# Issuing four of seven input loads late, from between GpSimd's row sums, in a sparse 3x3 convolution

## Chip, cores, metric

The kernel runs on one core of one Trainium2 chip. The metric is the device time of one execution in microseconds (us), as the median of several runs. A run is called fast or slow by its state: a slow run is over 1.5% above the fastest of the same kernel. Only fast runs enter a ratio; a median and its range are over all runs of a kernel, and where a slow one is among them the text says so.

## The reference

The convolution takes 16 images of 64 channels and 64x64 pixels, and 128 filters of 3x3 with one weight in ten kept. Everything is float32.

```
x_pad = np.pad(x, ((0, 0), (0, 0), (1, 1), (1, 1)))
for b, co, ci, kh, kw:
    if weight[co, ci, kh, kw] != 0:
        output[b, co] += weight[co, ci, kh, kw] * x_pad[b, ci, kh:kh+64, kw:kw+64]
```

The input is 16.8 MB, the weights 0.3 MB, and the output 33.6 MB. The kernel does not use the zeros; it computes a dense product in bf16.

## The kernel before

Two images form a pair, which fills 128 partitions (2 x 64 channels). There are 8 pairs, each in its own tile `xs[p]`, so a load never waits for a buffer to come free. GpSimd issues the loads because they cast float32 to bf16 on the way. Here all of them are issued at the start:

```python
    xs = [x_pool.tile([128, H, W], BF16, name=f"x{p}") for p in range(NP)]
    ...
    nc.sync.dma_start(out=x_head[:, 0:HEAD, :], in_=pair(0)[:, 0:HEAD, :])
    nc.gpsimd.dma_start(out=xs[0][:, HEAD:H, :], in_=pair(0)[:, HEAD:H, :])
    ...
    for p in range(1, NP):
        nc.gpsimd.dma_start(out=xs[p], in_=pair(p))

    ...                                   # idle matmuls, ahead of the first real ones
    for _ in range(27):
        nc.tensor.matmul(idle_ps, idle_rhs, idle_rhs, start=True, stop=True)
```

The first half of pair 0, the "head", comes as float32 through SyncE's queue and is cast by VectorE and ScalarE. A pair has 4 blocks of 16 rows. In 31 of the 32 blocks GpSimd first adds neighbouring rows (a "row sum"), TensorE multiplies, ScalarE and VectorE put the parts together in an output tile `o`; only pair 0's first block goes without a row sum. SyncE then stores the pair:

```python
    def twos(p, o, r0):
        s = s_pool.tile([128, 8, W], BF16, name="s")          # 3 buffers
        nc.gpsimd.tensor_tensor(out=s, in0=xs[p][:, r0 : r0 + 16 : 2, :],
                                in1=xs[p][:, r0 + 1 : r0 + 16 : 2, :], op=ADD)
        shared = product([(s, G1, 0, 1)], 8)
        ...
    for p in range(NP):
        o = [o_pool.tile([C_OUT, H, W], FP32, name="o") for _ in range(2)]   # 7 buffers
        last = p == NP - 1
        for blk in range(4):
            ...
                twos(p, o, r0)
            ...                    # of the last pair, each half is stored by itself
        if not last:
            for n in range(2):
                nc.sync.dma_start(out=out[2 * p + n], in_=o[n])
```

## Time and profile before

| what | value | where from |
|---|---|---|
| time | 127.82 us (127.75 to 128.02, 4 runs) | runs |
| span of the profiled run | 125.4 us (this run took 127.12 us) | page |
| TensorE, VectorE, GpSimd busy | 86%, 66%, 32% | page |
| the 16 DMA engines busy with q1 and q0 | 96.9% | page |
| last addition of VectorE ends | 111.8 us | chain of waits |
| last store has landed | 124.2 us | landing records |

The page is the summary of one profiled execution. In its lines PE is TensorE, PEld TensorE's loading of weights, DVE VectorE, ACT ScalarE, POOL GpSimd and SP SyncE; a q behind the name means the engine's instruction queue. L135 is line 135 of the kernel, `s<-x` writes tile `s` and reads tile `x`, and x36 counts instructions. PEclk, or the granted clock, is the share of TensorE's full clock that it was given.

The two queues are q1, which SyncE feeds (stores, weights, head), and q0, which GpSimd feeds (casting loads). One more view is needed: the page's list of transfers, with the size of each (an output store counted in float32, a load on its bf16 side) and the median time in us from issue to landing.

```profile
out_dram<-o SPq DMA_DIRECT2D x14, 2048.0 KB, 19.8
x<-in_x_dram POOLq DMA_DIRECT2D x7, 1024.0 KB, 29.3
out_dram<-o SPq DMA_DIRECT2D x4, 1024.0 KB, 12.3
```

A store of 2 MB takes some 5 us alone (an estimate: 2.1 MB at 421 GB/s, the rate over this whole kernel), yet 19.8 us pass from its issue: transfers stand in a queue.

### The profile page before, as it was taken

How to read it: one execution, taken by the hardware profiler on the slowest of the kernel's cores; microseconds unless marked ns; L12 is line 12 of the kernel's file. 1: busy time of each engine (PE TensorE's matmuls, PEld its weight loads, DVE VectorE, ACT ScalarE, POOL GpSimd, SP SyncE). 2: the span in 40 equal slices, each digit the busy share in tenths (PEclk: the TensorE clock that was granted, in tenths of full speed). 3: DMA queues.
4: the chain of work that ended last, by engine and by line, in shares of the span. 5: the costliest groups of instructions: out<-in, count | busy, mean ns of one | idle time of the engine just before them, and what ended most of it. 6: DMA issues, size and time to landing. Idle time of an engine off the chain costs nothing.

```text
span 125.4 us, 2486 instructions
## 1 busy us (share of the span) xinstructions
PE 107.5 (86%) x1002; PEld 58.8 (47%) x1002; DVE 82.4 (66%) x135; ACT 39.0 (31%) x71; POOL 40.7 (32%) x45
## 2 busy tenths in 40 slices
PE   6679999999999999999999999999999999920000
PEld 6435555555555555555555555555555555500000
DVE  0463877877787778777877787778777877760000
ACT  4555323333333333333333333333333333300000
POOL 6936533333333333333333333333333300000000
PEclk9999999999999999999999999999999999997555
DMA  5999999989999999999999999999999999999980
GB/s 146 338 222 220 212 214 220 191 259 350 324 311 337 308 293 319 342 316 308 426 429 423 408 429 434 450 416 434 418 418 429 429 444 423 434 397 423 423 369 10
DMA packets 4044, 42.93 MB, mean 342 GB/s; under 512 B 448, under 2 KB 448, under 8 KB 704
## 3 DMA queue, kind: packets, MB, share of 16 engines
q1 hardware_dynamic: 2880, 34.90, 66.2%
q0 software_dynamic: 1152, 7.86, 30.7%
q8 instruction: 8, 0.13, 0.4%
q14 instruction: 4, 0.03, 0.1%
HBM read 17.07 MB, written 33.55 MB: 404 GB/s over the span
## 4 chain that ended last, share of the span: by engine, by line
PE 81%; DMA 4%; DVE 1%; issue 1%; DVEq 0%; SPq 0%
PE ps L135 81%; DMA o<-in_x_dram 4%; DVE o L168 1%; DVEq L214 0%; DVE x L87 0%; SPq L60 0%; DVEq L168 0%
## 5 line engine op out<-in xcount | busy, mean ns | idle before, releaser
L168 DVE TENSOR_TENSOR o<-ps,pc 128x512 f32<-128x512 f32 x124 | 77.8, 686 | 22.1 <-PE ps L135 19.8
L135 PE MATMUL ps<-x,wT 64*128 64x504 bf16 (+3 forms) x780 | 88.8, 373 | 1.5 <-DVE x L87 1.5
L135 PEld LDWEIGHTS <-wT 64*128 64x128 bf16 x966 | 55.2, 94 | 49.4 <-issue 1.5
L154 POOL TENSOR_TENSOR s<-x 128x512 bf16<-128x512 bf16 x31 | 35.6, 1152 | 57.7 <-PE ps L135 41.5
L161 ACT COPY pc<-ps 128x512 f32<-128x512 f32 x62 | 33.3, 589 | 64.0 <-issue 61.8
L135 PE MATMUL ps<-s,wT 64*128 64x512 bf16 (+1 forms) x186 | 25.7, 377 | 0.0
L74 PE MATMUL ps<-idle_rhs 128*128 128x128 bf16 x27 | 3.1, 310 | 1.0 <-DVE idle_rhs L71 1.0
L67 POOL DMA_DIRECT2D x<-in_x_dram x7 | 3.7, 561 | 0.0
L74 PEld LDWEIGHTS <-idle_rhs 128*128 128x128 bf16 x27 | 2.8, 144 | 1.0 <-DVE idle_rhs L71 1.0
L91 DVE CAST w_bf<-w_sb 128x192 bf16<-128x192 f32 (+1 forms) x4 | 1.3, 382 | 3.0 <-DMA w_sb<-in_weight_dram 3.0
L149 DVE COPY o<-ps 128x512 f32<-128x512 f32 x2 | 1.4, 692 | 2.0 <-PE ps L135 2.0
L148 ACT COPY o<-ps 128x512 f32<-128x512 f32 x2 | 1.2, 586 | 2.4 <-PE ps L135 2.4
L87 ACT CAST x<-o 128x576 bf16<-128x576 f32 (+1 forms) x2 | 1.5, 802 | 0.5 <-DMA o<-in_x_dram 0.5
L91 ACT ACT_TABLE_LOAD x1 | 1.3, 1283 | 0.7 <-PEq L203 0.7
L97 PE MATMUL ps<-ident,w_bf 128*128 128x128 bf16 x9 | 1.1, 292 | 0.4 <-DVE w_bf L91 0.4
L87 DVE CAST x<-o 128x576 bf16<-128x576 f32 x1 | 0.5, 460 | 1.4 <-DMA o<-in_x_dram 1.4
L91 ACT CAST w_bf<-w_sb 128x64 bf16<-128x64 f32 (+1 forms) x2 | 0.7, 418 | 1.9 <-DMA w_sb<-in_weight_dram 1.9
L97 PEld LDWEIGHTS <-w_bf 128*128 128x128 bf16 x9 | 0.8, 128 | 0.8 <-DVE w_bf L91 0.8
L101 DVE TENSOR_TENSOR wT<-ps,wT 128x384 bf16<-128x384 f32 x2 | 1.0, 550 | 0.0
L63 POOL DMA_DIRECT2D x<-in_x_dram x1 | 0.7, 696 | 0.8 <-POOLq L203 0.8
L71 DVE MEMSET idle_rhs<- 128x64 uint32 x1 | 0.1, 112 | 0.8 <-PEq L203 0.8
L110 ACT CAST wT<-ps 128x384 bf16<-128x384 f32 x1 | 0.5, 481 | 0.4 <-PE ps L97 0.4
(8 smaller groups left out, 1.9 us busy)
## 6 DMA issues: line engine op xcount, KB each, us to landing
out_dram<-o SPq DMA_DIRECT2D x14, 2048.0 KB, 19.8
x<-in_x_dram POOLq DMA_DIRECT2D x7, 1024.0 KB, 29.3
out_dram<-o SPq DMA_DIRECT2D x4, 1024.0 KB, 12.3
o<-in_x_dram SPq DMA_DIRECT2D x1, 1024.0 KB, 5.4
x<-in_x_dram POOLq DMA_DIRECT2D x1, 512.0 KB, 7.5
w_sb<-in_weight_dram SPq DMA_DIRECT2D x1, 288.0 KB, 3.1
```

Of the source, the lines that this page charges most:

```text
L67: nc.gpsimd.dma_start(out=xs[p], in_=pair(p))
L74: nc.tensor.matmul(idle_ps, idle_rhs, idle_rhs, start=True, stop=True)
L87: copy(out=xs[0][:, a:b, :], in_=x_head[:, a:b, :])
L91: copy(out=w_bf4[:, g, a:b, :], in_=w_v[:, k : k + b - a, :])
L97: nc.tensor.matmul(wps[:, j, :], src, ident, start=True, stop=True)
L101: nc.vector.tensor_tensor(out=wT[:, g], in0=wps, in1=wT[:, G1], op=SUB)
L135: nc.tensor.matmul(ps[n][:, lo:hi, c_lo:c_hi], tap(g, kw, n), src[q, a:b:step, c_lo + kw - 1 : c_hi + kw - 1], start=(i == 0), stop=(i == ...
L148: nc.scalar.copy(out=o[0][:, r0 : r0 + rows, :], in_=ps[0])
L149: nc.vector.tensor_copy(out=o[1][:, r0 : r0 + rows, :], in_=ps[1])
L154: nc.gpsimd.tensor_tensor(out=s, in0=xs[p][:, r0 : r0 + 16 : 2, :], in1=xs[p][:, r0 + 1 : r0 + 16 : 2, :], op=ADD)
L161: nc.scalar.copy(out=c, in_=shared[n])
L168: nc.vector.tensor_tensor(out=o[n][:, first : r0 + 16 : 2, :], in0=ps[n], in1=pc[n], op=ADD)
```

## The change

The intent is to let the first stores have the DMA engines to themselves: pairs 4 to 7, which nobody needs before about 50 us, are no longer loaded at the start. Each is loaded while the pair three places ahead of it is computed.

```diff
-    for p in range(1, NP):
+
+    def load(p):
         nc.gpsimd.dma_start(out=xs[p], in_=pair(p))
+
+    EARLY = 4
+    for p in range(1, EARLY):
+        load(p)
@@ in the loop over pairs and blocks
                 twos(p, o, r0)
+                if p > 0 and blk == 1 and p + EARLY - 1 < NP:
+                    load(p + EARLY - 1)
```

## The prediction

> **What bounds the kernel now.** I read the page first: the span, the busy rows, the DMA queues.
>
> ```profile
> span 125.4 us, 2486 instructions
> ...
> PE   6679999999999999999999999999999999920000
> ...
> DMA  5999999989999999999999999999999999999980
> ...
> q1 hardware_dynamic: 2880, 34.90, 66.2%
> q0 software_dynamic: 1152, 7.86, 30.7%
> ...
> HBM read 17.07 MB, written 33.55 MB: 404 GB/s over the span
> ```
>
> TensorE looks like the bound, full from slice 4 to slice 36. But its row ends at about 112 us, and the DMA row is full from slice 2 to slice 39. The queue shares say it in one number: q1 (SyncE's transfers) and q0 (GpSimd's) together keep the 16 DMA engines busy for 96.9% of the span, 121.5 of 125.4 us. The chain of waits, in order of time, ends like this (start, length, what):
>
> ```profile
> 7.12 102.09 PE ps L135 x954
> ...
> 111.16 0.60 DVE o L168
> ```
>
> The chain stops at 111.76 us and the span at 125.4: in the last 13.6 us no engine computes, and only stores drain. The page's "PE 81%" follows the computation to the last issue of a store; it doesn't say what delayed that store's landing. Next I cut the span into stretches of 3 us. Columns: stretch, length, busy time (count) of PE, its weight loads, DVE, ACT, POOL; then granted clock, DMA share, GB/s.
>
> ```profile
> 15.00:18.00 3.00, 3.00 (x30) 1.60 (x28) 2.27 (x5) 1.07 (x2) 1.15 (x1) 1.00 1.04 216
> ...
> 36.00:39.00 3.00, 3.00 (x32) 1.57 (x29) 2.27 (x5) 1.07 (x2) 1.16 (x1) 1.00 1.04 333
> ...
> 66.00:69.00 3.00, 3.00 (x31) 1.60 (x28) 2.27 (x5) 1.07 (x2) 1.15 (x1) 1.00 1.03 437
> ...
> 114.00:117.00 3.00, 0.00 (x0) 0.00 (x0) 0.00 (x0) 0.00 (x0) 0.00 (x0) 0.59 1.01 426
> ```
>
> The DMA share is 1.0 in every stage: loads alone (15 us), loads beside stores (36), stores alone with TensorE running (66), stores alone after it (114). The rates look different only because q0 casts float32 to bf16 and its bytes are counted on the bf16 side: 7.86 MB in q0 stand for 15.7 MB read. Counted on the float32 side, 216 is 432 GB/s, like the 426 to 437 of the stores. So one resource is full at one rate from start to end, and **the time is set by the DMA engines' total work**. TensorE would matter only if it left them without work.
>
> The work: 50.63 MB in HBM bytes. The share of 0.43 in the first stretch (0 to 3 us) puts its start at about 1.7 us, that of 0.62 in 120 to 123 its end at about 121.9. That is 120.2 us, 421 GB/s, or 2.374 us for each MB. The last landing record, at 124.2 us, comes 2.3 us later, then the program's end.
>
> **What the Trainium skill says.**
> - "DMA: Bandwidth & Descriptors", section "Issuing engines are not separate DMA queues": transfers started by different engines run on the same 16 DMA engines and interleave. The trace agrees: in the packet records of 36 to 60 us a 16 KB packet takes 624 ns on either queue, and the two together move about 422 GB/s, what one moves alone. Moving a load from early to late gives stores bandwidth earlier and takes as much away later.
> - The same page, section "Measured": a 16 MB load reaches 425 GB/s. Here 421 over the whole kernel: no rate is left to gain by a better order.
> - "Perfetto Trace Analysis", section "Per-instruction lifecycle: what the profiler-reported window actually captures": for a GpSimd transfer the profiled interval ends with the descriptors, not with the data. The trace agrees: 561 ns for each issue, 29.3 us median to landing.
> - "SBUF — State Buffer", section "SBUF: two separate sides", the box on VectorE and GpSimd's descriptors: a two-port VectorE instruction keeps GpSimd from writing them. The four moved issues will stand beside L168, a two-input addition from PSUM, not one of the copies that the box warns of. No issue of the kernel before stands beside L168, so its trace is silent here.
>
> **The change part by part.** GpSimd's instruction order in the built kernel confirms the diff: after three row sums of pair 0 and two of pair 1 comes the load of pair 4, then the loads of 5, 6, 7, each after the second row sum of pairs 2, 3, 4. Nothing is removed or added: 8 issues and 31 row sums remain, and TensorE's, VectorE's and ScalarE's work is the same. When would the loads be issued? GpSimd's timeline in the kernel before (start, length, what, idle before):
>
> ```profile
> 13.77 1.15 POOL L154 TENSOR_TENSOR s<-x 128x512 bf16<-128x512 bf16 x1 [2.21 <-DMA x<-in_x_dram]
> 15.16 1.15 POOL L154 TENSOR_TENSOR s<-x 128x512 bf16<-128x512 bf16 x1 [0.23 <-PE ps L135]
> 18.40 1.15 POOL L154 TENSOR_TENSOR s<-x 128x512 bf16<-128x512 bf16 x1 [2.09 <-PE ps L135]
> ...
> 27.97 1.15 POOL L154 TENSOR_TENSOR s<-x 128x512 bf16<-128x512 bf16 x1 [2.10 <-PE ps L135]
> ```
>
> The row at 13.77 is pair 1's first block, that at 15.16 its second, so load 4 goes out at 15.16 + 1.15 = 16.3 us. Pair 2's second is at 27.97 (load 5 at 29.1), pairs 3 and 4 follow 12.8 us apart (41.9 and 54.7).
> - GpSimd: 4 x 0.56 us leave the start, where it then idles 2.0 us anyway waiting for ScalarE's cast, and come back one at a time in front of row sums with 2 us of idle time before them. Worth 0.
> - Deadlines: the row sums that first read pairs 4 to 7 start at 50.3, 63.1, 75.9 and 88.8. A load is 2.10 MB, 5 us alone, 10 us at half share. Load 4 should land near 30, the others near 41, 54, 67. At least 20 us to spare: TensorE won't wait.
> - DMA: does it ever run dry? I add up issued work. A pair's load is 4.98 us, a pair's stores (4.19 MB) 9.96. Up front: weights and pairs 0 to 3, 8.68 MB, 20.6 us, from 1.7 to 22.3. Stores of a pair are issued at 21.6 and then every 12.8 us, as now; the last pair's two halves at 104.7 and 111.2.
>
> ```
> issued at    what        work is queued until   left just before
>  16.3        load 4       27.3                   6.0
>  21.6        stores 0     37.2                   5.7
>  29.1        load 5       42.2                   8.1
>  34.4        stores 1     52.2                   7.8
>  41.9        load 6       57.1                  10.3
>  47.2        stores 2     67.1                   9.9
>  54.7        load 7       72.1                  12.4
>  60.0        stores 3     82.0                  12.1
>  72.8        stores 4     92.0                   9.2
>  85.6        stores 5    101.9                   6.4
>  98.4        stores 6    111.9                   3.5
> 104.7        last, half  116.9                   7.2
> 111.2        last, half  121.9                   5.7
> ```
>
> The queue is never empty, and the smallest margin (3.5 us at 98.4) is there before the change too, since all loads have landed by then in both. The end is 121.9, as now. **Sum: 0 us.** What changes is only who lands first: the stores of pairs 0 to 2 some microseconds earlier, loads 4 to 7 later.
>
> **The rivals.**
> 1. *TensorE sets the end, and earlier stores shorten the tail.* For it: the 81%, and loads that no one needs for 30 us compete with the first stores. Were it true, the last stores (2.1 MB, 5 us) would start when issued, at 111.2, and land near 118.5: 5.7 us gained, 122.1 us. Against it: the 5.7 us of older stores queued at 111.2, which no order of loads removes.
> 2. *A DMA hole opens.* The first stores, issued at 21.6, move their first packet only at 25.8 by the packet records. If load 4 came late, the engines would stand from 22.3 to 25.8: up to 3.5 us lost, 131.3 us, slower by 2.7%. Against it: load 4 is issued 6 us before its turn and carries the engines to 27.3. A smaller hole, in single engines, I allow 0.5 us.
> 3. *Switching costs or gains.* From 23.5 to 26 us the packet records sum to 330 KB less than at 430 GB/s, 0.8 us. If several separate loads each bring such a dip, up to +2 us; if none does, -0.8.
> 4. *GpSimd's issue is slowed beside VectorE.* Even 5 us for an issue would only use the margin before row sums that lie 2 blocks ahead; nothing or almost nothing.
>
> **Range and chances.** My best guess is the time before, 127.82 us, plus 0.1 for rivals 2 and 3 taken together: 127.9. Runs of before spread over 0.2 us; with -0.8 and some +1 for the dips the range is 127.1 to 128.9. Over 2% faster needs below 125.3, which rival 1 alone could give: 0.03. Over 2% slower needs above 130.4, a full hole of rival 2 or many dips: 0.04. Within 2%: 0.93.
>
> **What would show it.** Right: DMA share 1.0 in every stretch from 3 to 120 us; the two queues' shares again sum to about 97%; TensorE's chain piece of about 102 us unchanged, with no wait on a load of x; GpSimd's issues in pairs 1 to 4 near 0.56 us each; loads land in a median of about 11 us instead of 29.3, whole-image stores in about 18 instead of 19.8; the last landing still 12 to 13 us after the last store is issued. Wrong: a stretch of DMA share well below 1 near 22 to 30 us (rival 2), a DMA total in us that grew (rival 3), or a span that ends nearer to TensorE's end (rival 1).

## The result

The changed kernel took 127.31 us (127.09 to 127.56, 4 runs), the kernel before 127.82 us. The ratio is 0.9958, with a 95% interval of 0.9937 to 0.998. Ratios here are the mean time of one kernel's fast runs over that of the other's in the same rounds, so they are not quite the ratio of the medians quoted. By the 2% rule the time is the same.

The page of the changed kernel, in the rows shown of before:

```profile
span 125.5 us, 2486 instructions
...
PE   6669999999999999999999999999999999990000
...
DMA  4999999999999999999999999999999999999980
...
q1 hardware_dynamic: 2880, 34.90, 66.3%
q0 software_dynamic: 1152, 7.86, 30.6%
...
HBM read 17.07 MB, written 33.55 MB: 403 GB/s over the span
```

The DMA row is as full as it was, and the queues' shares sum to 96.9% again. But the PE row reaches one slice further. The chain of waits of the changed kernel (start, length, what) tells by how much:

```profile
7.50 104.60 PE ps L141 x954
...
114.04 0.60 DVE o L174
```

TensorE's piece of the chain ended at 109.2 us before and ends at 112.1 now, and VectorE's last addition ends at 114.6 instead of 111.8. **Computation ended 2.9 us later, and the span is the same within 0.2 us.** The last landing is at 124.4 us (124.2 before). That alone says what kind of kernel this is: the tail of stores after the computation has shrunk by what the computation lost.

The delay is not spread out. GpSimd's timeline (start, length, what, idle before) shows the first late load and its neighbours:

```profile
18.05 1.15 POOL L160 TENSOR_TENSOR s<-x 128x512 bf16<-128x512 bf16 x1 [2.09 <-PE ps L141]
19.14 0.57 POOL L68 DMA_DIRECT2D x<-in_x_dram  x1
21.30 1.14 POOL L160 TENSOR_TENSOR s<-x 128x512 bf16<-128x512 bf16 x1 [1.59 <-PE ps L141]
```

The issue takes 0.57 us out of idle time: the next row sum had 1.59 us of idle time left before it, where others have 2.0 to 2.1. So GpSimd is not what came late. TensorE's timeline from its start shows it, first of the kernel before, then of the changed kernel:

```profile
4.46 1.12 PE L97 MATMUL ps<-ident,w_bf 128*128 128x128 bf16 x9 [0.41 <-DVE w_bf L91]
7.12 3.99 PE L135 MATMUL ps<-x,wT 64*128 64x512 bf16 x36 [1.54 <-DVE x L87]
```

```profile
4.21 1.22 PE L103 MATMUL ps<-ident,w_bf 128*128 128x128 bf16 x9 [0.16 <-DVE w_bf L97]
7.50 6.49 PE L141 MATMUL ps<-x,wT 64*128 64x512 bf16 x36 [2.07 <-DVE x L93]
```

The same first 36 products took 3.99 us before and 6.49 us now: TensorE started slowly, after standing idle for 2.07 instead of 1.54 us, and computed 2.5 us late from there on. (The other 0.4 us of the 2.9 are its later start, 7.50 instead of 7.12 us.) The list of waits has no load of x in it, for TensorE or for GpSimd.

Finally the list of transfers, and one stretch of 3 us (columns as in the prediction; the last two are DMA share and GB/s), both of the changed kernel:

```profile
out_dram<-o SPq DMA_DIRECT2D x14, 2048.0 KB, 15.9
x<-in_x_dram POOLq DMA_DIRECT2D x7, 1024.0 KB, 16.1
out_dram<-o SPq DMA_DIRECT2D x4, 1024.0 KB, 9.6
```

```profile
99.00:102.00 3.00, 3.00 (x34) 1.55 (x30) 2.48 (x4) 0.91 (x3) 0.99 (x2) 1.00 0.90 377
```

Stores land earlier after their issue and loads sooner after theirs, as they must if each waits behind less. In this stretch the DMA share is 0.90, against 1.01 in the kernel before: the queue of stores ran nearly dry, because pair 6's stores came 3 us late. (With the same order of loads and these stores on time, `after_warm` below loses nothing there.)

### The profile page after: what moved, and what is told of

It reads as the page before. It is cut to its first block, busy times and chain, and to the rows that moved or that the text cites. A ratio compares the mean times of both kernels' runs of the same rounds, so it can differ in the third digit from the quotient of the medians.

```text
span 125.5 us, 2486 instructions
## 1 busy us (share of the span) xinstructions
PE 110.1 (88%) x1002; PEld 57.2 (46%) x1002; DVE 82.3 (66%) x135; ACT 38.9 (31%) x71; POOL 40.6 (32%) x45
## 4 chain that ended last, share of the span: by engine, by line
PE 83%; DMA 5%; DVE 1%; issue 1%; DVEq 0%; SPq 0%
PE ps L141 83%; DMA o<-in_x_dram 5%; DVE o L174 1%; DVEq L224 0%; DVE x L93 0%; SPq L60 0%; DVEq L174 0%
## 5 line engine op out<-in xcount | busy, mean ns | idle before, releaser
L141 PE MATMUL ps<-x,wT 64*128 64x504 bf16 (+3 forms) x780 | 91.1, 381 | 2.1 <-DVE x L93 2.1
L141 PEld LDWEIGHTS <-wT 64*128 64x128 bf16 x966 | 53.6, 96 | 54.0 <-issue 4.9
## 6 DMA issues: line engine op xcount, KB each, us to landing
out_dram<-o SPq DMA_DIRECT2D x14, 2048.0 KB, 15.9
x<-in_x_dram POOLq DMA_DIRECT2D x7, 1024.0 KB, 16.1
```

What stands on the lines that cost most here:

```text
L141: nc.tensor.matmul(ps[n][:, lo:hi, c_lo:c_hi], tap(g, kw, n), src[q, a:b:step, c_lo + kw - 1 : c_hi + kw - 1], start=(i == 0), stop=(i == ...
```

## The experiments

Three questions were open. Does the DMA engines' work really set the time, although TensorE fills the chain? What happens where the queue does run dry? And is the gain of 0.4% real, and does it belong to the order of the loads? "Warm" kernels have 22 more idle matmuls between the weight transposes and the first product:

```diff
+    for _ in range(22):
+        nc.tensor.matmul(idle_ps, idle_rhs, idle_rhs, start=True, stop=True)
     difference(G01, ps0)
```

### What sets the time: less computation, and one store less

`thin_after` is the changed kernel with two of the three columns of taps, a wrong result:

```diff
-KW_ORDER = (1, 0, 2)
+KW_ORDER = (1, 0)
```

> The changed kernel with two of the three columns of taps (a wrong result on purpose): a third of TensorE's work and of its time per pair is gone, all transfers stay. TensorE theory (the end of computation sets the time): 30 us less or more, about 94 to 98 us. DMA theory: the same 50.63 MB still have to pass, so 126.7 to 127.7 us, with TensorE standing idle on buffers of o that wait for stores.

`thin_skip` is the same with one image's store left out, also wrong:

```diff
-            for n in range(2):
+            for n in range(2 if p != 3 else 1):
                 nc.sync.dma_start(out=out[2 * p + n], in_=o[n])
```

> As thin_after, and one store of 2.10 MB of the 16 images is left out (wrong result on purpose). DMA theory: 4.98 us less than thin_after, since the queue never runs dry: 121.8 to 122.7 us. TensorE theory: no change against thin_after.

`thin_after` took 126.16 us (126.08 to 126.23), ratio to the kernel before 0.9878. `thin_skip` took 121.49 us (121.43 to 121.51), ratio 0.9512. The PE and DMA rows of `thin_after`, and the end of its chain of waits:

```profile
PE   6669999999999999119995499999997000000000
...
DMA  4999999999999999999999999999999999999991
```

```profile
96.89 1.20 DVE o L174 x2
```

From its list of waits (who waited for what: total us, times, longest):

```profile
DVE o L174 <- DMA out_dram<-o: 9.1, 2, 5.5
```

TensorE has holes now (VectorE waits for tiles of `o` whose stores haven't landed, and TensorE waits behind it) and VectorE is done at 98.1 us, 16.5 us earlier than in the changed kernel. The time fell by 1.2 to 1.5 us, depending on the run of the changed kernel that one compares with, not by 30. One store of 2.10 MB less took 4.67 us off (4.98 expected). So **bytes set the time, and computation hardly enters**. Both kernels came out somewhat under their expected ranges. What `thin_after` gained on the changed kernel lies after 100 us in the table of losses below: 0.55 us where the changed kernel's queue runs low, and 0.6 us because the engines finish closer together.

### Where the queue runs dry: fewer loads up front

`early2` and `early3` load only one or two pairs up front besides pair 0, and the later ones one or two pairs ahead.

```diff
-    EARLY = 4
+    EARLY = 2        # early3: EARLY = 3
```

> Only pair 1 is loaded up front (with pair 0), and every later load is issued one pair ahead. DMA theory: the work issued up front is 4.49 MB, 10.7 us, so the engines run dry at about 12.4 us and start again about 1 us after GpSimd's next issue at 16.3 (or 19.1, where the first products are slow): a hole of 5 to 8 us, and the time rises by as much, to 132 to 136 us, with perhaps 1 to 3 us more where a row sum waits for its load. The theory that there is slack in the DMA queue because TensorE is the bound: 127 to 129 us, only what TensorE waits.

> Two pairs loaded up front besides pair 0, every later load two pairs ahead. DMA theory: 6.58 MB up front, 15.6 us, keep the engines busy to 17.3 us; load 3 is issued at 16.3 us if TensorE starts fast (hole 0 to 1 us) and at 19.1 if it starts slowly (hole about 3 us). Then the loads have 20 us or more until they are read and take about 15 us beside stores, so TensorE does not wait. Time 127.3 to 128.3 with the fast start, 129.5 to 131 with the slow one. Theory that lateness alone costs (each load later makes the time longer): between the changed kernel's 127.5 and early2's 140.9, about 132 to 134.

`early3` took 130.28 us (129.69 to 131.16), ratio 1.0206, as expected for a slow start of TensorE. Its stretches from 15 to 24 us show the hole that the second rival of the prediction describes:

```profile
15.00:18.00 3.00, 3.00 (x31) 1.50 (x29) 1.90 (x4) 0.83 (x3) 1.02 (x1) 1.00 0.90 188
18.00:21.00 3.00, 3.00 (x30) 1.52 (x28) 2.27 (x5) 1.04 (x2) 1.66 (x2) 1.00 0.38 38
21.00:24.00 3.00, 3.00 (x32) 1.57 (x30) 2.27 (x5) 1.07 (x2) 1.14 (x1) 1.00 0.84 167
```

The column GB/s counts loads on the bf16 side; loads alone run at 216. The three stretches lack 28, 178 and 49 GB/s, on the float32 side twice that: 2 x 3 us x 255 GB/s = 1.53 MB, or 3.6 us at 428 GB/s. TensorE computed without a wait for a load, as in the changed kernel.

The same sum can be made for the whole of each profiled run from its packet records: in each part of the span, the length of the part less the bytes moved in it (float32 side) at 428 GB/s, which is the time that the engines lost there. Since all these kernels move the same bytes, the span has to be about 122.0 us plus the losses; the table says where each kernel lost.

```
us lost in         start   5 to 24  24 to 35  35 to 100  100 to 120  120 to last   sum   span
                   to 5                                              packet
before              0.77     0.01      0.75      0.06        0.02        1.75      3.37  125.4
before_again        0.86    -0.01      0.85      0.08        0.02        1.84      3.63  125.6
before_warm         0.81     0.05      0.77      0.03        0.02        2.11      3.79  125.8
before_warm2        0.78     0.01      0.70      0.04        0.02        1.98      3.53  125.5
changed             0.84    -0.01      0.68      0.09        0.47        1.48      3.54  125.5
after_again         0.82    -0.01      0.99      0.09        0.20        1.42      3.50  125.5
after_warm          0.83    -0.02      0.79      0.05        0.02        1.66      3.33  125.3
after_warm2         0.72     0.20      0.72      0.04        0.02        2.22      3.92  125.9
early3              0.81     3.56     -0.02      1.50        0.01        1.67      7.53  129.4
early3_warm         0.89     1.65      0.22      1.22        0.01        1.11      5.11  127.1
thin_after          0.85     0.73      0.11     -0.01       -0.08        0.89      2.49  124.4
```

Each kernel has a loss of 0.7 to 0.9 us at the start, while the weights come in packets of 2304 bytes, one dip of 0.7 to 1.5 us soon after the two queues begin to run side by side (in `thin_after` before 24 us; in `early3` and `early3_warm` only from 33 us on, when the next load meets the stores), and one at the end, when the engines don't all finish at once. `early3` lost 4.0 us more than the changed kernel, and its span is 3.9 us longer: 3.6 us of it are the hole and 0.7 us its larger dip, less some 0.3 us by which it lost less from 100 us on. (Its profiled run was the slowest of the four, at 131.16 us; the median is 2.6 us above the kernel before of the same session.) **What the engines miss at the start comes back as time at the end.**

`early2` took 140.85 us (140.27 to 141.56), ratio 1.1038, which is 5 us over the 136 of its expectation and 2 us over the 139 that it allowed with waiting row sums. The hole is there (no packet from 14.3 to 19.3 us), but loads one pair ahead also come too late. By the same sum as in the table its engines lost 7.3 us from 5 to 24 us, as the expectation of the hole said, but also 3.3 us from 24 to 100 and 5.9 us after that. Two lines of its waits (who waited for whom: total us, times, longest):

```profile
POOL s L160 <- DMA x<-in_x_dram: 58.6, 6, 13.4
...
PE ps L141 <- POOL s L160: 13.0, 4, 5.4
```

A load that is issued while stores are queued took 13 to 16 us to land in these kernels, and a pair takes 12.8 us to compute. One pair ahead is therefore too little, and TensorE stood still for 13 us. This corrects a term of my prediction; see below.

### Is it the hole or the lateness?

`early3_warm` is `early3` with the idle matmuls, so that TensorE starts fast and GpSimd reaches the issue of load 3 earlier.

> early3 (130.28 us) with the same 22 idle matmuls. Its hole ran from 17.5 to 20.5 us, because the first products were slow and GpSimd issued load 3 at 19.2 us. With the fast start load 3 is issued at 16.6 us and its packets start about 1.3 us later, at 17.9: hole theory: 127.3 to 128.5 us, with a hole under 1 us. Theory that a load two pairs ahead is simply too late: still 130 or more.

It took 128.75 us (128.13 to 128.87), ratio 1.0071. The load was issued at 17.25 instead of 19.20 us, with the same distance of two pairs, and 1.5 us of the 2.6 us by which `early3` is slower than the kernel before are gone. So it is the hole and not the lateness. The expectation was a little low, because the load came 0.65 us later than it assumed and because it counted the idle time alone and not the slow ramp after it:

```profile
15.00:18.00 3.00, 3.00 (x32) 1.57 (x30) 2.27 (x5) 1.07 (x2) 2.77 (x3) 1.00 0.89 186
18.00:21.00 3.00, 3.00 (x32) 1.57 (x30) 2.27 (x5) 1.07 (x2) 1.14 (x1) 1.00 0.90 126
```

From 18 to 21 us the engines are busy for 90% of the time but move 126 GB/s instead of 216: their packets take longer (from 19 to 20 us a median of 791 ns, instead of 625 before the hole).

### Is the half microsecond real, and whose is it?

The unchanged kernels were run again, and both with the idle matmuls, in three sessions, each on another chip: first `before_again`, `after_again` and `after_warm`, then `before_warm`, then the other three.

> The kernel before, unchanged, timed against itself. Theory A (the measured gain of 0.4% is real and belongs to the order of the loads): ratio 1.000 within 0.2%. Theory B (it is a lottery of the chip or of the run): ratio anywhere from 0.995 to 1.005. The profile also shows whether the kernel before always gets its full TensorE rate from the first product on (24 matmuls between 7.1 and 9 us) or, as the changed kernel did in its profile, runs the first 36 products in 6.5 us instead of 4.0.

> The changed kernel, unchanged. Theory A: ratio 0.994 to 0.998 again, 0.5 us gained. Theory B: ratio within 0.998 to 1.002. If the slow first products (36 in 6.5 us) come from the change, they are there again and TensorE's last product ends near 113 us; if they are chance, it may end near 110.5. In both cases the DMA theory expects the span to stay within 0.5 us of 125.5.

> The changed kernel with 22 more idle matmuls between the weight transposes and the first product, so that TensorE does not stand idle for 2 us there. Expected by both theories: the first 36 products take 4.0 us, TensorE ends near 110 to 110.5 us instead of 112.9. DMA theory: the time stays within 0.6 us of the changed kernel (126.7 to 127.5), because only the small dip of the DMA share near 101 to 103 us can close. TensorE theory (the end of computation sets the time): 2.4 us less, about 124.9.

> The kernel before with the same 22 idle matmuls that the changed kernel got in after_warm (127.08 us, 0.9954 of the kernel before). Both profiles of the kernel before already had fast first products. If the order of the loads is worth half a microsecond once TensorE starts alike, this one stays at the time of the kernel before, 127.6 to 127.8, ratio 0.999 to 1.001. If the half microsecond belongs to TensorE's start and not to the order, this one gains it too: 127.1, ratio 0.994 to 0.997.

> The changed kernel with 22 idle matmuls ahead of the first product, once more, now on the same chip and in the same rounds as the next two. If the order of the loads gains a little when TensorE starts fast: 127.1 us, 0.3 to 0.5 us under before_warm2. If the first reading was a matter of the chip: within 0.2 us of before_warm2.

> The kernel before with the same idle matmuls. Order theory: 127.5 to 127.7 us, ratio 0.998 to 1.000. Chip theory: the same as after_warm2 within 0.2 us.

> The changed kernel as it is. If its slow first products (36 in 6.5 or 5.7 us in both profiles so far) cost it what the order gains, it lies between the two above, 127.3 to 127.6 us, and its spread from run to run is wider than the 0.2 us of after_warm; if the order gains nothing, it is at 127.7 like the kernel before.

| run | median us (lowest to highest) | ratio to the kernel before, 95% interval | idle before the first product, us | first 36 products, us |
|---|---|---|---|---|
| kernel before, first | 127.82 (127.75 to 128.02) | 1 | 1.54 | 3.99 |
| changed, first | 127.31 (127.09 to 127.56) | 0.9958 [0.9937, 0.998] | 2.07 | 6.49 |
| before_again | 127.75 (127.38 to 127.94) | 1.0006 [0.9984, 1.0029] | 1.92 | 3.99 |
| after_again | 127.65 (127.26 to 127.81) | 0.9996 [0.9974, 1.0018] | 2.71 | 5.67 |
| after_third | 127.51 (126.98 to 131.69) | 0.998 [0.9956, 1.0004] | slow run | slow run |
| before_warm | 127.54 (127.3 to 127.86) | 0.9987 [0.9973, 1.0001] | 0.73 | 3.99 |
| before_warm2 | 127.41 (127.36 to 129.9) | 0.9981 [0.9964, 0.9999] | 0.82 | 3.99 |
| after_warm | 127.08 (126.93 to 127.11) | 0.9954 [0.9934, 0.9975] | 0 | 3.99 |
| after_warm2 | 127.37 (127.11 to 128.84) | 0.9997 [0.9952, 1.0042] | 0.46 | 3.99 |

The medians and ranges of `after_third` and `before_warm2` take in a slow run each (131.69 and 129.9); without it the medians are 127.46 and 127.40.

The gain is not stable. The changed kernel itself gave 0.9958, 0.9996 and 0.998, and the warm version 0.9954 in one session and 0.9997 in a later one. `after_again` came out as theory B said. The cleanest test, `after_warm2` beside `before_warm2` on one chip and in the same rounds, has the medians 0.04 us apart, as the chip theory said, and not 0.3 to 0.5. `before_warm` came out just under the first of its two forecasts, far from the second. The medians of the changed and the warm kernels lie 0 to 0.6 us below that of the kernel before in the same session (fast runs), but the interval of the changed kernel includes 1 in two of three sessions. What I can say is that the order of the loads is worth between nothing and half a percent, and **its cause stays open**. The table of losses shows where runs differ: in the last part, with 1.4 to 2.2 us until the slowest engine has finished. The changed kernels are at 1.42, 1.48, 1.66 and 2.22 there, the four of before at 1.75 to 2.11, and the changed kernel without idle matmuls gives 0.2 to 0.5 us back at 100 to 120 us, where its queue runs low. That is too few profiles to call it an effect of the order. The wide interval of `after_warm2` comes from one run of 128.84 us that just counts as fast.

Two things of this group can be said. First, TensorE's start. The idle time before it is what passes between the last weight transpose and the cast of the head. In the table, and in `early2` (2.19 us idle, 5.54 us for the products), `early3` (2.01 and 6.66) and `early3_warm` (1.39 and 3.99), starts after 1.92 us or less were fast and those after 2.01 us or more slow. But `thin_after` breaks this rule: it started slowly after 1.82 us,

```profile
7.32 4.01 PE L141 MATMUL ps<-x,wT 64*128 64x512 bf16 x24 [1.82 <-DVE x L93]
```

with 167 ns for each product instead of 111 (3.99 us for 36). The record of the granted clock in the packed traces says more. In every fast start it begins with the full clock, granted between 3.99 and 6.61 us and kept until the computation is over. In `after_again` the full clock comes at 4.78 us, falls to half at 8.20 and returns at 11.61, as the page's PEclk row shows in its third and fourth slices:

```profile
PEclk9986999999999999999999999999999999999755
```

It is the same in `early2` (half from 7.10 to 10.51 us) and `thin_skip` (7.33 to 10.74). In the changed kernel, `early3` and `thin_after` there is no record at all before 12.62, 12.86 and 10.00 us, and the products become fast within 0.2 us of these times; the 1.00 that the page and the stretches print for the time before them only stands for a missing record. So the slow start is a matter of when the clock is granted, which the idle time alone doesn't tell. The slow start was there in all four fast profiles of full kernels with late loads and no extra idle matmuls, and in neither of the kernel before; whether the change causes that, six profiles don't show. Second, it matters little for the time: `after_warm`'s chain of waits has its TensorE piece back at the old length,

```profile
7.47 102.09 PE ps L143 x954
...
111.50 0.60 DVE o L176
```

and computation ends 2.5 us earlier than in the changed kernel, for 0.2 us less of span in the profiles (125.3 against 125.5) and 0.1 to 0.6 us less in the medians of the same session (127.37 and 127.51, 127.08 and 127.65).

## Why the prediction was right

**The bound.** Right. The prediction put the time down to the total work of the DMA engines against a page that gives TensorE 81% of the chain. `thin_after` (computation done 16.5 us earlier, time 1.2 to 1.5 us shorter) and `thin_skip` (2.10 MB less, 4.67 us less) show it. So does the profile of the change itself, where computation ended 2.9 us later at the same span.

**The sum of 0 us.** Right: 127.31 to 127.65 us in three sessions, for 127.9 predicted and a range of 127.1 to 128.9. The extra 0.1 us had the wrong sign, within the noise.

**GpSimd's part.** Right: 0.57 us for each of the four issues, now beside VectorE's additions, as against 0.56 at the start without them, and taken out of idle time. The times of issue were 2.9 us later than predicted (19.1, 31.9, 44.8, 57.6 instead of 16.3, 29.1, 41.9, 54.7), 2.5 us of it TensorE's slow start and the rest the later head. In `after_warm2`, with a fast start, they are 16.7, 28.9, 41.7 and 54.5.

**The queue that never runs dry.** Almost right, and with less margin than the table said. It gave 3.5 us at 98.4, the stores of pair 6. Those stores came about 3 us late, and the DMA share fell to 0.90 for one stretch, a loss of 0.3 us (0.5 us over 100 to 120 us). The prediction took the start of TensorE as fixed, which it isn't: the sign "TensorE's chain piece of about 102 us unchanged" failed, with 104.60. That a delay of 2.9 us still fitted into a margin of 3.5 is luck. That the table carries weight is shown by `early3`, where one entry of it, load 3, was issued at 19.2 us, after the engines had run out of work at about 18, and cost 2.6 us in the median.

**The time of a load to land.** Here a term was mis-sized: "5 us alone, 10 us at half share", and a median of about 11 us (its own deadlines, near 30, 41, 54 and 67 us, already made 12 to 14). It was 16.1 us, and the four landed at 31.5, 47.1, 60.8 and 73.8. In the packet records, the three last loads (issued at 31.9, 44.8 and 57.6) send their first packet 4.3 to 4.6 us after the issue, pass for 9.5 to 10 us at half share, and have landed 2 to 3 us after their last packet started. I had only the middle part. It changed nothing here, since each of the four landed 17 us or more before its first row sum (load 7: 73.8 and 91.6), but it is what made `early2` slower than I expected. The stores' median came out at 15.9 us instead of 18.

**The last landing** "12 to 13 us after the last store is issued" was wrong: 9.7 us (114.7 to 124.4), because the issue moved with the computation and the landing stayed.

**The rivals.** The first, that earlier stores shorten the tail, fell: the last store was issued later and still landed when it did before. The second, a hole, is real, as `early3` and `early2` show, but three pairs up front are enough to avoid it. Of the third, the late loads brought no further dips: in half-microsecond steps the packet records of the changed kernel have one stretch below 400 GB/s between 5 and 100 us, at 26 to 28.5, when the first stores set in, like the kernel before at 23.5 to 26.5. (The prediction's 330 KB for 23.5 to 26 us were rather 290 to 300, or 0.7 us. A second stretch, at 101.5 to 102.5, is the queue running low.) The fourth didn't appear.

## What to carry to other kernels

Where the DMA engines are busy from start to end, reordering transfers only decides who lands first. Add up the bytes, divide by the rate, and look for moments at which the queue would be empty; those came back as time here. Of the rest of the order, only loads that came too late for the computation (`early2`) and a larger dip (`early3`) cost something. A chain of waits that ends in computation long before the span does is the sign to look at the transfers behind it. And a load issued beside a busy queue of stores needs its wait in the queue added to its transfer time, so issue it, in a kernel like this one, about two computed pairs ahead and not one.

## What the Trainium skill lacked or had wrong

- "DMA: Bandwidth & Descriptors", section "Queues, rings and completion order", says that an engine goes round its queues packet by packet. One would expect a transfer on an empty queue to get its share at once. In these runs it didn't: a load issued by GpSimd beside queued stores sent its first packet 3.6 to 4.6 us after its issue (once 6.0, the last of `early2`), the first stores 3.4 to 4.3 us after theirs where the loads beside them still ran for 6 us or more. Where the load beside them was over within 2.3 to 2.6 us, the first stores took 1.3 to 1.5 us (`early2`, `early3`, `early3_warm`), and with idle engines a load took 1.3 us (`early3`, issued at 19.20, first packet at 20.48). The page's specifications give about 1 us to the first byte of a GpSimd transfer, which is near the last figure; it gives none for a transfer that meets another queue's work.
- No page that I read has the dip soon after the two queues begin to run side by side: 0.7 to 1.5 us of transfer lost in each kernel of the table (at 23.5 to 26.5 us in the kernel before), with the engines busy: the packets of loads took a median of 841 ns there, and 624 from 36 to 60 us. Nor has one the ramp after a hole: 126 instead of 216 GB/s for 3 us in `early3_warm`, at a DMA share of 0.90.
- "TensorE: Matmul & The Clock Gate", Part 1, has the array at full clock after a busy window of about 3.4 us and at half after an idle one, in windows that run freely. The records agree on the length: each half-clock stretch at the start lasts 3.41 us (`after_again`, `early2`, `thin_skip`). What the page lacks is how much of a window has to be idle: in these three, gaps of 2.71, 2.19 and 2.17 us, shorter than a window, were followed by half clock, and the 1.92 us of `before_again` were not.
